# Mixture-of-experts stage: second blocks in four short branches, overflow in one branch at the end, a named ring of weights

## The chip, the core and the metric

The kernel runs on one core of a Trainium2 chip. The time is that of one execution on the device, in microseconds. Before the change it is 1266.83 us, the median of three runs (1257.88 to 1268.67).

## The reference

One layer of an encoder on 1024 tokens of width 1024, all in float32: differential attention, then a mixture of 16 experts, and a last RMSNorm. The change is in the experts:

```python
g_idx = jnp.argmax(g_logits, axis=-1)                       # one of 4 groups per token
top_v, top_i = lax.top_k(e_sel, EXPERT_TOP_K)               # 2 of its 4 experts
hid = jax.nn.silu(jnp.einsum('td,edf->tef', t, w_gate)) * jnp.einsum('td,edf->tef', t, w_up)
hid = hid * gates.astype(hid.dtype)[:, :, None]             # gate is 0 for experts not chosen
y = jnp.einsum('tef,efd->td', hid, w_down)
```

Each expert has three weights of 1024 x 512. A token's two experts add to one output row. Which tokens go to which expert is known only at run time; in all there are 2048 pairs of token and expert, and the routing of these inputs gives the experts 0 to 15: 102, 114, 97, 119, 153, 119, 191, 127, 98, 114, 103, 149, 153, 151, 133 and 125 tokens.

## The kernel before

**Stages.** Attention and routing fill the time up to about 763 us. The experts' stage follows, expert by expert, and at its end the last RMSNorm of all rows.

**Rows of tokens.** The normed tokens lie in DRAM as `h2d`, the residual sums as `accd`, each with 128 spare rows behind the 1024. `slots` and `slots_mm` make, two experts ahead, the list of row numbers of an expert (`idx`) and its gate weights (`tt`); a slot without a token gets a spare row's number. `gather` (an indirect DMA issued by POOL) fetches the rows of the first block (128 slots) and of the second (`M2` = 64 slots), `xpose` turns the first block into `XT`, and `scatter_add` adds the result to `accd`.

**Weights.** An expert's weights come in `NP` = 12 pieces of 128 x 1024 float32: 0 to 3 are the gate and up halves of the first 256 hidden columns, 4 to 7 of the other 256, 8 to 11 the down rows. `load_raw` has SP issue the load into one of `NRAW` raw tiles `wraw`. To multiply with nearly full precision, each piece is split: `split_hi` (ACT) casts it to `whi`, `split_lo` (DVE; pieces 8 and 11, the tuple `PLO`, on POOL) subtracts to give `wlo`. These lie in `NSLOT` = 14 pairs of tiles that the pool hands out in turn. Each split lets SP load the piece that is `NRAW` later.

**One expert.** `block` runs 48 matmuls of gate and up (`gu`) for the first 256 hidden columns, then 48 for the others; `gate` (ACT's SiLU, DVE's product) makes `sl`, `hid` transposes it on PE and splits it, `down` runs 12 matmuls per half into `py0` and `py1`. Work for other experts is put in by hooks, pairs of a count and a call: when the matmuls of `gu` reach that count, the call is written. `SPL` holds the counts of the splits, `EVAC` that of the previous expert's evacuation, `XPH`, `OH` and `SMM` those of the next experts' transposes and lists. ACT, DVE and POOL keep the order in which the calls are written, and PE too (`manual_schedule`); each engine works its own instructions in order and waits on semaphores for the others.

**The second block.** Where an expert has more than 128 tokens, its further ones (up to 64) run through the same weights with two terms instead of three, with hi and lo side by side in one 128-wide operand. This is one branch, `tc.If(n > P, label="small%d")`, taken by each engine for itself on the expert's count, and it is long: it holds the second block and the first block's down matmuls between its parts, and behind them `over_loop`, a loop over tokens past 192 in a branch of its own. The other side, `arm.Else()`, holds the first block's down matmuls alone. Two splits (`NARM`) stand in both sides, two more behind the branch. `mark_branch_hint_location` has PE told ahead where the branch is.

Of the kernel before, what the change touches and what calls it, by code (L numbers as in the profile page):

```python
# [35 lines left out]
def build(tc, x, c, ada_w, ada_b, norm_mix, norm_ffn, w_in, lq1, lk1, lq2, lk2, subln, w_out,  # L36
# [1027 lines left out]
    NRAW = 12  # L1064
# [34 lines left out]
    nslot = [0]  # L1099
# [39 lines left out]
    def split_done(n):  # L1139
# [43 lines left out]
    pos1, io1, pj, njn, mhalf, cnt, gates, oh = (RT0[n] for n in ("pos1", "io1", "pj", "njn", "mhalf", "cnt", "gates", "oh"))  # L1183
# [96 lines left out]
    def small_pe(xg):  # L1280
        pt = mps.tile([P, KT, M2], F32, name="xt", bufs=2)
# [95 lines left out]
    def gate(pg, g, R, lo=None):  # L1377
# [338 lines left out]
```

## Time and profile before

| | |
|---|---|
| Median of three runs | 1266.83 us |
| The profiled execution | 1261.08 us, span 1259.3 us, mean granted clock 0.955 |
| PE busy | 1115.3 us (89%) |
| DVE busy | 946.1 us (75%) |
| ACT, POOL busy | 733.6 us (58%), 383.5 us (30%) |
| Moved by DMA | 205.25 MB, mean 163 GB/s |

The profile has busy times of each engine, the waits with what ended them, and the instructions in order of time. PE is TensorE's matmuls and PEld its loads of weights, which overlap; PEldq, DVEq and so on are the sequencers, which branch, wait and issue. [...] Experts are counted from 0.

### The profile page before, as it was taken

What the parts mean: (1) busy time and instruction counts of PE and PEld (TensorE: products, weight loads), DVE (VectorE), ACT (ScalarE), POOL (GpSimd) and SP (SyncE); (2) the same over time, 40 slices, a digit from 0 to 9 for tenths busy, and PEclk for the clock granted to TensorE, in tenths of its full rate; (3) what the DMA queues carried; (4) which work ended last, traced back from release to release, by engine and by line L of the source; (5) the groups of instructions that cost most, each with busy time, mean ns of one, the idle gap of its engine ahead of it and who ended that gap; (6) DMA issues with size and microseconds to landing.
All of it is one profiled execution on the core that took longest, in us unless ns stands there. A gap on an engine that the chain in (4) does not pass through costs nothing. (4 is left out here: it accounts for less than half of the span.)

```text
span 1259.3 us, 18790 instructions
## 1 busy us (share of the span) xinstructions
PE 1115.3 (89%) x6760; PEld 926.5 (74%) x6760; DVE 946.1 (75%) x1500; ACT 733.6 (58%) x1220; POOL 383.5 (30%) x335
## 2 busy tenths in 40 slices
PE   4989999999999999998989967988898788898883
PEld 3657777777777777776778866877797677787772
DVE  5869788887889686789765477798777677677754
ACT  5566766666676667677554233666464555545544
POOL 3011110111111020115014125456364554545532
PEclk9899999999999999998999987999999998999996
DMA  9622033332223010124148536899797899679737
GB/s 329 196 67 64 26 91 91 92 93 80 88 89 93 30 37 15 42 66 129 69 125 284 172 130 215 276 317 344 200 314 225 271 292 321 185 218 267 199 101 273
DMA packets 153280, 205.25 MB, mean 163 GB/s; under 512 B 11652, under 2 KB 122917, under 8 KB 153138
## 3 DMA queue, kind: packets, MB, share of 16 engines
q1 hardware_dynamic: 146432, 179.86, 44.6%
q0 software_dynamic: 6512, 23.06, 7.7%
q8 instruction: 77, 1.26, 0.4%
q10 hardware_dynamic: 194, 0.54, 0.1%
q14 instruction: 65, 0.53, 0.1%
HBM read 175.77 MB, written 27.67 MB: 162 GB/s over the span
## 5 line engine op out<-in xcount | busy, mean ns | idle before, releaser
L1119 DVE TENSOR_TENSOR wlo<-wraw,whi 128x1024 fp32r<-128x1024 f32 x155 | 221.6, 1479 | 25.9 <-ACT whi L1114 15.4
L1373 PE MATMUL gu<-whi,XT 128*128 128x256 f32 x1216 | 211.1, 286 | 4.3 <-DVEq L1462 3.3
L1114 ACT CAST whi<-wraw 128x1024 fp32r<-128x1024 f32 x192 | 188.4, 1049 | 23.4 <-PE py L1405 17.8
L486 ACT ACTIVATE E<-E,mn 128x1024 f32<-128x1024 f32 x128 | 147.1, 1151 | 84.0 <-DVE mn L483 83.7
L1373 PEld LDWEIGHTS gu<-whi,XT 128*128 128x128 f32 x1216 | 175.6, 194 | 8.1 <-ACTq L1462 5.3
L483 DVE CUSTOM_DVE_ANT_0 E<-S,negd 128x1024 f32<-128x1024 f32 x128 | 152.8, 1220 | 19.3 <-PE S L478 18.6
L1373 PE MATMUL gu<-wlo,XT 128*128 128x256 f32 x704 | 152.0, 294 | 15.9 <-DVE wlo L1119 14.2
L143 POOL TENSOR_TENSOR wl<-wraw,wh 128x1024 fp32r<-128x1024 f32 x21 | 50.6, 2409 | 326.0 <-ACT wh L142 285.6
L285 PE MATMUL mm<-hH,wh 128*128 128x512 f32 x336 | 139.3, 415 | 2.1 <-DVE V L384 2.1
L285 PE MATMUL mm<-hL,wh 128*128 128x512 f32 x336 | 140.2, 417 | 0.0
L285 PE MATMUL mm<-hH,wl 128*128 128x512 f32 x336 | 138.7, 413 | 0.0
L1373 PEld LDWEIGHTS gu<-wlo,XT 128*128 128x128 f32 x704 | 111.6, 194 | 20.3 <-DVE wlo L1119 17.8
L1119 POOL TENSOR_TENSOR wlo<-wraw,whi 128x1024 fp32r<-128x1024 f32 x37 | 97.2, 2631 | 94.4 <-ACT whi L1114 94.4
L513 ACT CAST aH<-tp 128x512 fp32r<-128x512 f32 x128 | 74.0, 578 | 74.7 <-PE tp L511 74.4
L1405 PE MATMUL py<-whi,hid 128*128 128x512 f32 x256 | 96.2, 434 | 12.8 <-issue 10.2
L497 DVE SCALAR_TENSOR_TENSOR E<-E,r 128x1024 f32<-128x1024 f32 x64 | 85.8, 1341 | 27.8 <-ACT E L495 26.3
L514 DVE TENSOR_TENSOR aL<-tp,aH 128x512 fp32r<-128x512 f32 x128 | 88.0, 687 | 16.0 <-ACT aH L513 14.8
L511 PE MATMUL tp<-ident,E 128*128 128x128 f32 x512 | 78.6, 276 | 11.5 <-DVE aL L514 8.3
L511 PEld LDWEIGHTS tp<-ident,E 128*128 128x128 f32 x512 | 62.4, 142 | 35.0 <-DVE aL L514 15.4
L693 PE MATMUL mm<-wo,wh 128*128 128x512 f32 x240 | 80.1, 408 | 1.3 <-ACT mm L705 1.3
L285 PEld LDWEIGHTS mm<-hH,wh 128*128 128x128 f32 x336 | 63.4, 189 | 18.3 <-issue 5.1
L285 PEld LDWEIGHTS mm<-hL,wh 128*128 128x128 f32 x336 | 63.4, 189 | 17.1 <-issue 8.2
(346 smaller groups left out, 2337.8 us busy)
## 6 DMA issues: line engine op xcount, KB each, us to landing
wraw<-in_expert_w_gate SPq DMA_DIRECT2D x64, 512.0 KB
wraw<-in_expert_w_up SPq DMA_DIRECT2D x64, 512.0 KB
wraw<-in_expert_w_down SPq DMA_DIRECT2D x64, 512.0 KB
aw<-in_ada_w SPq DMA_DIRECT2D x64, 256.0 KB
wraw<-in_attn_w_in SPq DMA_DIRECT2D x23, 512.0 KB
ld<-in_ada_w SPq DMA_DIRECT2D x32, 256.0 KB
ld<-in_x SPq DMA_DIRECT2D x8, 512.0 KB
xt<-in_x SPq DMA_DIRECT2D x8, 512.0 KB
```

The costliest lines, as they stand in the source:

```text
L285: nc.tensor.matmul(pq, w[:, k], t[k][:, n], start=(k == 0 and i == 0), stop=(k == KT - 1 and i == 2))
L483: nc.vector.tensor_tensor_reduce(out=e, in0=sps[m], in1=negd[:, w0:w0 + S], op0=OP.add, op1=OP.min, scale=-slope, scalar=3.0e38, accum_out=mn)
L486: nc.scalar.activation(e, e, AF.Exp, bias=mn, scale=-1.0, accum_out=sm)
L497: nc.vector.scalar_tensor_tensor(es[0], es[1], r2, es[0], op0=OP.mult, op1=OP.add)
L511: nc.tensor.transpose(pt[:, i], a[:, k * P:(k + 1) * P], ident)
L513: nc.scalar.copy(th[:, kk * 4:kk * 4 + 4, q], pt)
L514: nc.vector.tensor_tensor(tl[:, kk * 4:kk * 4 + 4, q], pt, f(th[:, kk * 4:kk * 4 + 4, q]), op=OP.subtract)
L693: nc.tensor.matmul(py, w[:, h], wt[h][:, ns], start=(h == 0 and s == 0), stop=(h == H - 1 and s == 2))
L1114: nc.scalar.copy(WP[e, i][0], RAW[e, i])
L1119: eng.tensor_tensor(low, RAW[e, i], f(high), op=OP.subtract)
L1373: nc.tensor.matmul(pg[:, i], XT[:, xi, k], w[:, k % 4], start=(k == 0 and xi == 0 and wi == 0 and i == 0), stop=(k == KT - 1 and (xi, wi) ...
L1405: nc.tensor.matmul(py[n], hT[:, xi, i], WP[e, 8 + hf * 2 + i][wi][:, n * 512:(n + 1) * 512], start=(hf == 0 and j == 0), stop=(hf == 1 and ...
```

## The change

- The long branch goes. The first block's down matmuls, the splits and the evacuation stand outside any branch. The second block is cut into four short branches: its transposes (behind the gate/up matmuls), its first gate/up half (behind the first down half), its second gate/up half with the first down half (behind the second), and its second down half with the addition to `accd`, at the count `DSM` = 12 of the next expert. There is no other side and no hint.
- Six splits of the next expert stand between these branches, six at the counts of `SPL`; all low halves but two at the start of the stage are on DVE. The evacuation's second half moves from ACT and POOL to DVE.
- Tokens past 192 of all experts are one branch behind everything (`rest`), on the largest count `cmax`; it loads weights again and norms all rows again. The last expert's second block is `small15`.
- The slots are 14 named pairs in a list `RING`. Raw tiles are 11 instead of 12.
- Gathers and additions leave out slots whose row number is past 1023 (`bounds_check`). Counts in `OH`, `SMM`, `EVAC` and `N0` change.

```diff
-    NRAW = 12
+    NRAW = 11
     NRAW1 = 8
     NEARLY = 3
     CNT = 62
     XPH = (74, 86)
-    SMM = 80
-    OH = 40
-    NARM = 2
+    SMM = 92
+    OH = 66
...
+    RING = []
     def slot_tiles():
-        pool, nb = (mwr, NEARLY) if nslot[0] % NSLOT < NEARLY else (mw, NSLOT - NEARLY)
-        nslot[0] += 1
-        return [pool.tile([P, 1024], F32R, name=n, bufs=nb) for n in ("whi", "wlo")]
+        j = nheld[0] % NSLOT
+        if j == len(RING):
+            pool = mwr if j < NEARLY else mw
+            RING.append([pool.tile([P, 1024], F32R, name="%s%d" % (n, j)) for n in ("whi", "wlo")])
+        return RING[j]
...
-        eng = eng or (nc.gpsimd if i in PLO else nc.vector)
+        eng = eng or nc.vector
...
-    PLO = (8, 11)
-    EVAC = 52
-    N0 = 20
-    SPL = [(0, split_hi, 4), (0, split_lo, 4), (0, split_hi, 5), (0, split_lo, 5), (2, split_hi, 6), (3, split_hi, 7),
-           (30, split_lo, 6), (48, split_hi, 8), (48, split_lo, 8), (50, split_lo, 7), (50, split_hi, 10), (50, split_lo, 10),
-           (69, split_hi, 9), (70, split_lo, 9), (72, split_hi, 11), (80, split_lo, 11)]
+    EVAC = 60
+    DSM = 12
+    N0 = 28
+    SPL = [(0, 6), (24, 7), (56, 8), (64, 9), (80, 10), (90, 11)]
...
-    def gather(idx, b, tag, xg=None):
+    def gather(idx, b, xg=None):
         if xg is None:
-            xg = mg.tile([P, D], F32, name="xg" + tag, tag=tag)
-        m = M2 if b else P
-        nc.gpsimd.indirect_dma_start(out=xg[:m], out_offset=None, in_=h2d,
-                                     in_offset=bass.IndirectOffsetOnAxis(ap=idx[:m, b:b + 1], axis=0))
+            m, xg = (M2 if b else P), xg0[b]
+            nc.gpsimd.indirect_dma_start(out=xg[:m], out_offset=None, in_=h2d,
+                                         in_offset=bass.IndirectOffsetOnAxis(ap=idx[:m, b:b + 1], axis=0),
+                                         bounds_check=S - 1, oob_is_err=False)
+            return xg
...
-                                     in_=yo, in_offset=None, compute_op=OP.add)
-    def over_tiles(e):
-        if e < NE - 2:
-            return None, mp.tile([P, D], F32, name="yo")
-        return (mp.tile([P, D], F32, name="xc", tag="yo") if e == NE - 2 else raw_tile()), XG[e, 1]
-    def over_finish(e, ix, R, xc, yo):
-        if e < NE - 1:
-            scatter_add(ix[:R], yo[:R])
-        if e >= NE - 2:
-            xc, yo = xc[:R], yo[:R]
-            v.tensor_tensor(xc, xc, yo, op=OP.add)
-            sq = ss_tile()[:R]
-            nc.scalar.activation(yo, xc, AF.Square, accum_out=sq[:, 0:1])
-            r = rstd_of(sq, R)
-            v.scalar_tensor_tensor(xc, xc, r, nfin[0][:R], op0=OP.mult, op1=OP.mult)
-            out_rows(ix[:R], xc)
-    def over_block(e, XT, ix, g, R, lo=None):
-        xc, yo = over_tiles(e)
-        if xc is not None:
-            acc_rows(ix[:R], xc[:R])
+                                     in_=yo, in_offset=None, bounds_check=S - 1, oob_is_err=False,
+                                     compute_op=OP.add)
...
+    def small15(XT, ix, g):
+        e, R, xs = NE - 1, M2, XG[NE - 1, 1]
+        small_evac(small_pe(xs), XT)
+        xc = raw_tile()
+        acc_rows(ix, xc[:R])
+        block_steps(e, XT, g, R, xs, xs)
+        xc, yo = xc[:R], xs[:R]
+        v.tensor_tensor(xc, xc, yo, op=OP.add)
+        sq = ss_tile()[:R]
+        nc.scalar.activation(yo, xc, AF.Square, accum_out=sq[:, 0:1])
+        r = rstd_of(sq, R)
+        v.scalar_tensor_tensor(xc, xc, r, nfin[0][:R], op0=OP.mult, op1=OP.mult)
+        out_rows(ix, xc)
+    def rest(XT):
+        xl, yo = XG[NE - 1, 1], mp.tile([P, D], F32, name="yo")
+        for e in range(NE):
+            base = P + M2 if e < NE - 1 else 0
+            tc.no_sync_barrier()
+            with tc.If(cnts[e] > base):
+                for i in range(NP):
+                    load_raw(e, i)
+                    WP[e, i] = RING[i]
+                    nc.scalar.copy(RING[i][0], RAW[e, i])
+                    v.tensor_tensor(RING[i][1], RAW[e, i], f(RING[i][0]), op=OP.subtract)
+                v.memset(bs, float(base))
+                with tc.For_i(base, cnts[e], P):
+                    ix, tx = slots_mm(e, 1, slots(e, 1, base=bs))
+                    gather(ix, 0, xl)
+                    block_steps(e, run(xpose(xl, XT)), tx[:, 0, 3:4], P, yo)
+                    scatter_add(ix[:, 0:1], yo)
+                    v.tensor_scalar(bs, bs, float(P), None, op0=OP.add)
+        jk[0] = mp.tile([P, D], BF, name="jk", tag="hs")
+        for t in range(TB):
+            norm_load(t)
+            norm_sum(t)
+            rstds(t, t + 1)
+            norm_store(t)
...
+            tc.no_sync_barrier()
+            with tc.If(cnts[e] > P, label="small"):
+                small15(XT, idx[:M2, 1:2], tt[:, 1, 3:4])
+            tc.no_sync_barrier()
+            with tc.If(cnts[NE] > P + M2):
+                rest(XT)
+            return
+        upto(199)
-        tc.no_sync_barrier()
-        with tc.If(n > P, label="small%d" % e) as arm:
-            pt = small_pe(XG[e, 1])
-            g = tt[:, 1, 3:4]
-            xs = XG[e, 1]
-            if last:
...
-                s1 = gate(pg1, tt[:, 0, 3:4], P)
-                small_evac(pt, XT)
-                d = down(e, py, 0, h0, P)
-                take(d, 7)
-                h1 = hid(s1, P)
-                run(d)
-                spy = [mps.tile([P, 512], F32, name="spy%d" % n, tag="xt", bufs=2) for n in range(2)]
-                splits()
...
-                scatter_add(idx[:M2, 1:2], oyo[:M2])
-            over_loop(e, XT, n)
-        if last:
-            return
-        with arm.Else():
-            s1 = gate(pg1, tt[:, 0, 3:4], P)
-            d = down(e, py, 0, h0, P)
-            take(d, 7)
-            h1 = hid(s1, P)
-            splits()
...
+        g = tt[:, 1, 3:4]
+        xs = XG[e, 1]
+        def small(what):
+            tc.no_sync_barrier()
+            with tc.If(n > P):
+                what()
+        def splits(k):
+            split_to(nsplit[0] + k)
+        s1 = gate(pg1, tt[:, 0, 3:4], P)
+        pt = small_pt()
+        small(lambda: small_evac(small_pe(xs, pt), XT))
+        d = down(e, py, 0, h0, P)
+        take(d, 9)
+        h1 = hid(s1, P)
+        run(d)
+        splits(2)
+        sl, hs = mp.tile([P, 256], F32, name="sl"), mp.tile([P, 2, 2, P], F32R, name="hs")
+        pg = gu_tile()
+        small(lambda: gate(run(gu(e, XT, 0, M2, pg=pg)), g, M2, xs[:, 0:512], sl))
+        splits(2)
+        run(down(e, py, 1, h1, P))
+        pg2 = gu_tile("idx")
+        spy = [mps.tile([P, 512], F32, name="spy%d" % n, tag="xt", bufs=2) for n in range(2)]
+        def small_c():
+            hid(sl, M2, hT=hs)
+            gate(run(gu(e, XT, 1, M2, pg=pg2)), g, M2, xs[:, 512:1024], sl)
+            run(down(e, spy, 0, hs, M2))
+            hid(sl, M2, hT=hs)
+        def small_d():
+            for n in range(2):
+                run(down(e, spy, 1, hs, M2, (n,)))
+                fold(spy, oyo, n)
+                r = slice(n * 512, (n + 1) * 512)
+                v.tensor_tensor(oyo[:M2, r], oyo[:M2, r], g2b[:M2, r], op=OP.mult)
+            scatter_add(idx[:M2, 1:2], oyo[:M2])
+        small(small_c)
+        splits(2)
+        later.append((DSM, lambda: small(small_d)))
...
-            v.tensor_tensor(yo[:, 0:512], py[0], g2b[:, 0:512], op=OP.mult)
-            if e == NE - 2:
-                v.tensor_tensor(yo[:, 512:1024], py[1], g2b[:, 512:1024], op=OP.mult)
-            else:
-                nc.scalar.copy(yo[:, 512:1024], py[1])
-                nc.gpsimd.tensor_tensor(yo[:, 512:1024], yo[:, 512:1024], g2b[:, 512:1024], op=OP.mult)
+            for n in range(2):
+                v.tensor_tensor(yo[:, n * 512:(n + 1) * 512], py[n], g2b[:, n * 512:(n + 1) * 512], op=OP.mult)
...
-            tc.mark_branch_hint_location("small%d" % e, cnts[e] > P, engines=[mybir.EngineType.PE])
+            if e == NE - 1:
+                cnts[NE] = nc.values_load(cmax[0:1], min_val=0, max_val=S)
+                tc.mark_branch_hint_location("small", cnts[e] > P, engines=[mybir.EngineType.PE])
...
-            for c, what, i in SPL:
-                hooks.append((c, lambda e=e, i=i, what=what: what(e, i)))
-            hooks.append((SPL[-1][0], lambda: split_done(8)))
+            hooks += [(c, lambda: split_to(nsplit[0] + 1)) for c, i in SPL]
```

What moves, at three places. POOL, from the second gather of expert 1 to its next load of a count, first before (`wlo` is a weight's low half, `yo` the evacuated first block, `oyo` the second block's result):

```order
L1261 DMA xgxb<-h2d,ix 64x1024
L1119 TENSOR_TENSOR wlo<-wraw,whi 128x1024
L1577 TENSOR_TENSOR yo<-yo,g2b 128x512
L1419 DMA accd<-yo,ix 1152x1024
L1628 TENSOR_LOAD rk
```

and of the change:

```order
L1263 DMA xgxb<-h2d,ix 64x1024
L1540 COMPARE_AND_BRANCH
L1431 DMA accd<-oyo,ix 1152x1024
L1540 UNCONDITIONAL_BRANCH
L1540 ISA
L1540 UNCONDITIONAL_BRANCH
L1431 DMA accd<-yo,ix 1152x1024
L1631 TENSOR_LOAD rk
```

The split and the product are gone, and POOL passes a branch instead.

DVE, from the first block's second gate product of expert 0 (`sl`) into expert 1, before (the other side of the long branch):

```order
L1386 SCALAR_TENSOR_TENSOR sl<-sl,tt,gu 128x256
L1396 TENSOR_TENSOR hid<-tp,hid 128x256
L1119 TENSOR_TENSOR wlo<-wraw,whi 128x1024 x2
L1518 UNCONDITIONAL_BRANCH
L1119 TENSOR_TENSOR wlo<-wraw,whi 128x1024 x5
L1229 TENSOR_SCALAR rk<-rk 128x192 x8
L1386 SCALAR_TENSOR_TENSOR sl<-sl,tt,gu 128x256
L1119 TENSOR_TENSOR wlo<-wraw,whi 128x1024 x2
L1572 TENSOR_TENSOR yo<-py_7408,g2b 128x512
L1628 TENSOR_LOAD rk
L1396 TENSOR_TENSOR hid<-tp,hid 128x256
```

and of the change, from the same product:

```order
L1398 SCALAR_TENSOR_TENSOR sl<-sl,tt,gu 128x256
L1540 COMPARE_AND_BRANCH
L1299 TENSOR_TENSOR XT<-xt,XT 128x4x64 x2
L1540 UNCONDITIONAL_BRANCH x2
L1408 TENSOR_TENSOR hid<-tp,hid 128x256
L1122 TENSOR_TENSOR wlo_7650<-wraw,whi_7649 128x1024
L1122 TENSOR_TENSOR wlo_7656<-wraw,whi_7655 128x1024
L1540 COMPARE_AND_BRANCH
L1395 TENSOR_TENSOR xgxb<-xgxb,gu 64x512
L1398 SCALAR_TENSOR_TENSOR sl<-sl,tt,xgxb 64x256
L1540 UNCONDITIONAL_BRANCH x2
L1122 TENSOR_TENSOR wlo_6492<-wraw,whi_6491 128x1024
```

```order
L1122 TENSOR_TENSOR wlo_6500<-wraw,whi_6499 128x1024
L1122 TENSOR_TENSOR wlo_7291<-wraw,whi_7290 128x1024
L1122 TENSOR_TENSOR wlo_7294<-wraw,whi_7293 128x1024
L1540 COMPARE_AND_BRANCH
L1428 TENSOR_TENSOR oyo<-oyo,spy_7723 64x512
L1573 TENSOR_TENSOR oyo<-oyo,g2b 64x512
L1428 TENSOR_TENSOR oyo<-oyo,spy_7724 64x512
L1573 TENSOR_TENSOR oyo<-oyo,g2b 64x512
L1540 UNCONDITIONAL_BRANCH x2
L1122 TENSOR_TENSOR wlo_7297<-wraw,whi_7296 128x1024
L1398 SCALAR_TENSOR_TENSOR sl<-sl,tt,gu 128x256
L1122 TENSOR_TENSOR wlo_7389<-wraw,whi_7388 128x1024
```

Splits that stood behind one another now stand in pairs between the branches, and of the evacuation both halves are on DVE.

PE, from the last gate/up matmuls of expert 0 to the down matmuls, before and of the change (`xt` are the second block's transposes, `py` the down products):

```order
L1373 MATMUL gu<-wlo,XT 128x256 x2
L1373 MATMUL gu<-whi,XT 128x256 x2
L1518 COMPARE_AND_BRANCH
L1283 MATMUL xt<-ident,xgxb 128x64 x8
L1405 MATMUL py_7408<-whi,hid 128x512
```

```order
L1385 MATMUL gu<-whi_7388,XT 128x256
L1385 MATMUL gu<-whi_7392,XT 128x256
L1540 COMPARE_AND_BRANCH
L1292 MATMUL xt<-ident,xgxb 128x64 x8
L1540 UNCONDITIONAL_BRANCH x2
L1417 MATMUL py_7408<-whi_7434,hid 128x512
```

The first branch now ends behind the eight transposes; before, the down matmuls lay inside.

## Rows read from the trace of the kernel before

**Rows 1.** The page, busy us of each engine (share of the span)

```profile
PE 1115.3 (89%) x6760; PEld 926.5 (74%) x6760; DVE 946.1 (75%) x1500; ACT 733.6 (58%) x1220; POOL 383.5 (30%) x335
```

**Rows 2.** Nine stretches of the experts' stage: length, then busy us by engine

```profile
core 0: us, PE busy (x) PEld busy (x) DVE busy (x) ACT busy (x) POOL busy (x), PEclk, DMA share, GB/s
763.00:791.40 28.40, 23.08 (x151) 21.43 (x150) 18.83 (x23) 13.66 (x21) 15.92 (x23) 0.82 0.64 216
791.40:860.50 69.10, 59.94 (x445) 53.78 (x445) 59.57 (x76) 43.17 (x64) 41.04 (x39) 0.98 1.02 310
814.80:837.50 22.70, 19.53 (x149) 17.49 (x148) 20.99 (x26) 14.64 (x22) 12.30 (x12) 1.00 1.05 312
860.50:895.20 34.70, 31.97 (x241) 28.67 (x239) 24.95 (x35) 18.41 (x31) 14.10 (x14) 1.00 0.79 259
895.20:922.30 27.10, 22.68 (x148) 20.88 (x149) 21.41 (x26) 16.16 (x23) 18.30 (x16) 0.87 0.99 286
922.30:955.40 33.10, 31.92 (x241) 28.82 (x241) 22.42 (x35) 17.92 (x31) 15.50 (x13) 1.00 0.76 238
955.40:1062.60 107.20, 85.33 (x593) 76.50 (x593) 79.71 (x101) 59.03 (x86) 60.37 (x55) 0.90 0.97 293
1062.60:1208.80 146.20, 130.45 (x946) 116.68 (x944) 100.63 (x131) 76.03 (x122) 62.29 (x50) 0.99 0.74 213
763.00:1241.20 478.20, 408.77 (x2883) 366.41 (x2881) 346.13 (x442) 264.07 (x399) 244.09 (x219) 0.94 0.84 254
```

**Rows 3.** Waits of PE from 762 us: us in total, times, longest

```profile
PE tp L1392 <- DVE sl L1386: 18.8, 7, 3.8
PE gu L1373 <- DVE wlo L1119: 14.2, 14, 3.0
PE py L1405 <- issue: 10.2, 3, 4.5
PE py L1405 <- POOLq L1518: 9.3, 4, 5.8
PE py L1405 <- POOL wlo L1119: 4.1, 2, 2.5
PE gu L1373 <- DVEq L1462: 3.3, 5, 0.8
```

**Rows 4.** Branches of PE's sequencer, two lines: ns min/median/max

```profile
L1518 PEldq COMPARE_BRANCH  x16: 84/384/6532, 783.6 to 1237.1; - x16
L1462 PEldq COMPARE_BRANCH  x12: 187/354/3772, 891.3 to 1208.4; - x12
```

**Rows 5.** PE in order of time, expert 10: start, us, idle before

```profile
1054.13 0.77 PE L1405 MATMUL py<-whi,hid 128*128 128x512 f32 x1 [4.46 <-issue]
```

**Rows 6.** Waits of SP's queue, 762 to 1242 us

```profile
SPq L1093 <- DVEq L1462: 60.8, 5, 14.2
```

**Rows 7.** DVE in order of time, expert 3

```profile
836.26 6.99 DVE L1119 TENSOR_TENSOR wlo<-wraw,whi 128x1024 fp32r<-128x1024 f32 x6
...
844.99 5.30 DVE L1119 TENSOR_TENSOR wlo<-wraw,whi 128x1024 fp32r<-128x1024 f32 x2
```

**Rows 8.** POOL in order of time, expert 3

```profile
844.57 2.42 POOL L1119 TENSOR_TENSOR wlo<-wraw,whi 128x1024 fp32r<-128x1024 f32 x1 [5.20 <-ACT whi L1114]
846.94 2.27 POOL L1577 TENSOR_TENSOR yo<-yo,g2b 128x512 f32<-128x512 f32 x1
```

**Rows 9.** Groups by line: us, mean ns of one

```profile
L1572 DVE TENSOR_TENSOR yo<-py,g2b 128x512 f32<-128x512 f32 x15 | 10.2, 681 | 1.0 <-DMA xgxa<-h2d,ix 1.0
```

**Rows 10.** PE in order of time, end of expert 4's branch

```profile
894.01 0.63 PE L1405 MATMUL py<-whi,hid 128*128 128x512 f32 x2
895.24 0.47 PE L1373 MATMUL gu<-whi,XT 128*128 128x256 f32 x2 [0.60 <-DVEq L1462]
```

**Rows 11.** DMA queues, 814.8 to 860.5 us: packets, MB, share of 16 engines

```profile
q0 software_dynamic: 679, 2.45, 20.7%
```

**Rows 12.** POOL in order of time, the end

```profile
1252.37 1.06 POOL L1311 DMA_INDIRECT out<-yo,ix  x1 [7.87 <-POOLq L1518]
```

More of the change, by code (lines that the diff above doesn't have):

```diff
@@ L1182, in build @@
     v = nc.vector
-    pos1, io1, pj, njn, mhalf, cnt, gates, oh = (RT0[n] for n in ("pos1", "io1", "pj", "njn", "mhalf", "cnt", "gates", "oh"))
+    pos1, io1, pj, njn, mhalf, cnt, gates, oh, cmax = (RT0[n] for n in ("pos1", "io1", "pj", "njn", "mhalf", "cnt", "gates",
+                                                                        "oh", "cmax"))
     xg0 = [mg.tile([P, D], F32, name="xg" + n, tag=n) for n in ("xa", "xb")]
@@ L1278, in xpose, with small_pt, small_pe @@
         return XT
-    def small_pe(xg):
-        pt = mps.tile([P, KT, M2], F32, name="xt", bufs=2)
+    def small_pt():
+        return mps.tile([P, KT, M2], F32, name="xt", bufs=2)
+    def small_pe(xg, pt=None):
+        pt = small_pt() if pt is None else pt
         for k in range(KT):
@@ L1375, in gu, with gate @@
         return pg
-    def gate(pg, g, R, lo=None):
-        sl = mp.tile([P, 256], F32, name="sl")
+    def gate(pg, g, R, lo=None, sl=None):
+        sl = mp.tile([P, 256], F32, name="sl") if sl is None else sl
         if R == M2:
@@ L1456, in over_block @@
                 v.tensor_tensor(yo[:, r], py[n], g2b[:, r], op=OP.mult)
-        over_finish(e, ix, R, xc, yo)
-    def over_loop(e, XT, n):
-        tc.no_sync_barrier()
-        with tc.If(n > P + M2):
-            v.memset(bs, float(P + M2))
-            with tc.For_i(P + M2, n, P):
-                ix, tx = slots_mm(e, 1, slots(e, 1, base=bs))
-                xl = XG[e, 1]
-                gather(ix, 0, None, xl)
-                over_block(e, run(xpose(xl, XT)), ix[:, 0:1], tx[:, 0, 3:4], P)
-                v.tensor_scalar(bs, bs, float(P), None, op0=OP.add)
+    def small15(XT, ix, g):
[35 more added lines that the diff above has]
+            norm_store(t)
     def block(e, XT, idx, tt, hooks):
@@ L1505, in block @@
             finish15(ix, py, mp.tile([P, D], F32, name="yo"), XC[0])
-        else:
-            upto(199)
-        n = cnts[e]
-        nx = [divmod(j, NP) for j in range(nsplit[0], nsplit[0] + (0 if last else NARM))]
-        slots_to(nsplit[0] + len(nx))
-        def splits():
-            for j in nx:
-                split_hi(*j)
-                split_lo(*j)
-        tc.no_sync_barrier()
-        with tc.If(n > P, label="small%d" % e) as arm:
-            pt = small_pe(XG[e, 1])
-            g = tt[:, 1, 3:4]
-            xs = XG[e, 1]
-            if last:
-                small_evac(pt, XT)
-                over_block(e, XT, idx[:, 1:2], g, M2, xs)
-            else:
-                oyo = mp.tile([P, D], F32, name="yo") if e < NE - 2 else xs
-                s1 = gate(pg1, tt[:, 0, 3:4], P)
-                small_evac(pt, XT)
-                d = down(e, py, 0, h0, P)
-                take(d, 7)
-                h1 = hid(s1, P)
-                run(d)
-                spy = [mps.tile([P, 512], F32, name="spy%d" % n, tag="xt", bufs=2) for n in range(2)]
-                splits()
-                t0 = gate(run(gu(e, XT, 0, M2)), g, M2, xs[:, 0:512])
-                g1 = gu(e, XT, 1, M2, "idx")
-                take(g1, 24)
-                u0 = hid(t0, M2, "hs", 1)
-                t1 = gate(run(g1), g, M2, xs[:, 512:1024])
-                d = down(e, py, 1, h1, P)
-                run(down(e, spy, 0, u0, M2))
-                take(d, 4)
-                u1 = hid(t1, M2, "hs", 1)
-                take(d, 5)
-                run(down(e, spy, 1, u1, M2, (0,)))
-                fold(spy, oyo, 0)
-                run(down(e, spy, 1, u1, M2, (1,)))
-                fold(spy, oyo, 1)
-                run(d)
-                nc.gpsimd.tensor_tensor(oyo[:M2], oyo[:M2], g2b[:M2], op=OP.mult)
-                scatter_add(idx[:M2, 1:2], oyo[:M2])
-            over_loop(e, XT, n)
@@ L1553, in block @@
-        if last:
-            return
-        with arm.Else():
-            s1 = gate(pg1, tt[:, 0, 3:4], P)
-            d = down(e, py, 0, h0, P)
-            take(d, 7)
-            h1 = hid(s1, P)
-            splits()
-            run(d)
-            run(down(e, py, 1, h1, P))
-        split_done(NARM)
-        nx = [divmod(j, NP) for j in range(nsplit[0], nsplit[0] + (2 if e < NE - 2 else 0))]
-        for j in nx:
-            split_hi(*j)
-            split_lo(*j)
-        split_done(len(nx))
+            tc.no_sync_barrier()
```

35 lines of the change are left out of this document (19 added, 16 removed).

## Prediction

> **What bounds the kernel now.** I read the page first: PE is busy for 89% of the span [rows 1], and the chain of waits on it names only the last scatter, so it says nothing of the middle. Then I cut the experts' stage (763.0 to 1241.2 us) into one stretch per expert, by where a new expert's first gate/up matmul starts, and asked for busy times [rows 2]. The reader is to see three things. The stage takes 478.2 us, of which PE is busy 408.8: 69.4 us are idle. [...] The six with a second block last 34.7 + 33.1 + 146.2 = 214.0 us, of which expert 6 has 31.92 of PE work, 12.4 over an ordinary one. DVE and DMA stand close behind PE: in the third row DVE is busy 20.99 of 22.70 us and the DMA share is 1.05.
>
> So what can be won is PE's idle time and the clock. The waits of PE [rows 3] say who ends them: 18.8 us a transpose that waits for DVE's gate product, 14.2 a gate/up matmul that waits for DVE's low half of a weight, 9.3 + 4.1 a down matmul that waits for POOL (its skipped branch, and its two low halves per expert), 10.2 "issue", 3.3 the end of a small block's branch. "Issue" is the far jump over the small block: PE's sequencer needs 84 ns for the branch when it falls through and up to 6532 ns when it jumps [rows 4], and 4.46 us of one such jump stay visible [rows 5]. [...] And the loads of weights were held up by the long branch: SP's queue waited 60.8 us in five places for its end on DVE [rows 6].
>
> **The change, part by part.** *Far jump.* It is gone, with the Else side: -10.
>
> *POOL.* It splits no weights and multiplies no evacuation any more, so nobody waits there for it: -13. That work goes to DVE: two splits and a 512-wide product per expert. DVE's split takes 6.99/6 = 1.17 us by itself, but two of them took 5.30 us beside POOL's split and product, and POOL's run at the same time [rows 7, 8]. So DVE gets 2 x 1.17 + 0.68 [rows 9] = 3.0 us more and at least 5.30 - 2.33 = 3.0 us less: 21 us per ordinary expert, as now. ACT loses a copy and is not near the bound (14.64 us of 22.70).
>
> *Splits outside the branches.* Six of an expert's twelve splits now stand between the branches in the expert before, where loads follow each of them. What hangs on late DVE work is 18.8 + 14.2 = 33.0 us. I keep 8 of it: DVE at 21 us stays as full as PE, I count 0.4 us for each ordinary expert where PE reaches the second gate product before DVE does (an estimate from the order of the instructions), and 5 at both ends of the stage. That is -25; the bounds are 0 and -33.
>
> *Clock.* With no gap over 2.5 us left, the 11.7 us come back: -11.7. The first expert's clock is 0.82, but it starts out of idle time; nothing is counted.
>
> *End of the long branch.* -3.
>
> *Four skips.* Nine of experts 0 to 14 have no second block (those without a second-block matmul in the trace), so 36 branches are jumped. Each skipped body is replaced on PE, ACT and DVE by one instruction that waits for the engine's own last result. The nearest row is the skip of the old overflow loop at the end of a small block: the last down matmul pair runs from 894.01 to 894.64, the next matmul starts 0.60 us later [rows 10]; with the 0.16 us by which matmuls otherwise overlap, a skip costs PE 0.76 us. 36 x 0.76 = +27. The bounds: 0.25 (PE waits there anyhow for DVE) and 1.1 (as much again for the branch, median 0.354 us [rows 4]), so +9 to +40. [...]
>
> *Small block.* The same matmuls in the same number, 12.4 us on PE; the second half's transposes now come right after their gate product and stand uncovered: an estimate of 0.7 x 6 = +4 (0 to +8).
>
> *Fewer rows.* An ordinary expert moves 128 + 64 gathered and 128 added rows now. The reference's routing gives these experts 97 to 127 tokens, so about 218 rows stay. The software queue takes 20.7% of 16 engines' time over experts 2 and 3 (45.7 us), 4.7 us per expert [rows 11]; a third of it, 1.5 us, goes. I cost it at nothing: it brings the DMA from a share of 1.05 in 22.7 us to what fits in 22.4, which is what PE and DVE will need; without it DMA would be the bound at 23.8/1.05.
>
> *Ring, raw tiles.* The slots rotate as before; eleven raw tiles instead of twelve hold eleven twelfths of an expert, about 21 of 23 us, ahead. Nothing, as long as the DMA share stays under 1.05.
>
> *End.* The overflow of all experts is one branch behind everything, which is jumped on every engine; POOL's lies ahead of the last scatter's completion at 1252.37 [rows 12]. +3 (0 to +6.5, the longest jump).
>
> Sum: -10 -13 -25 -11.7 -3 +27 +4 +3 = -29. Counted by experts: ordinary ones 19.53 + 4 x 0.76 + 0.4 = 23.0, 8 of them 184 (-19); small ones 19.53 + 12.4 + 1.5 = 33.4, six of them 200 (-14); first and last +1: -32. I take -30. The profiled execution took 1261.1 us (span 1259.3), so 1231 for it; it lies 5.7 us under the median of the runs, 1266.8, which would give 1237. **I say 1234.**
>
> **Rivals.** *Slower: the short jumps fetch code.* If a jump on PE has to fetch its target, the sequencer needs 3.4 us and more (3772 and 6532 ns at most, medians 0.354 and 0.384, [rows 4]). Between two of the four branches stand only 12 down matmuls, some 2.8 us (two take 0.63 with 0.16 of overlap, so 0.235 each, [rows 10]), and the drain has emptied PE's queue: about 2.2 us of each fetch would show, and 2 us of clock behind it (11.7 us lost over some six gaps). If every third of the 36 jumps fetches (an assumption: the rows give medians and the longest alone), that is 12 x 4.2 = +50: 1234 + 50 = 1284. It decides from 10 jumps on. For it: four times as many branches. Against it: the bodies are short (8, 32, 44 and 8 matmuls, where the far jump passed over some 260). [...]
>
> *DVE stays late.* DVE too drains at four skips per ordinary expert, and it now has all splits; if the skips lengthen its cycle as they do PE's, the 33.0 us of waits stay: 1234 + 25 = 1259, no change that can be told. For it: DVE at 20.99 of 22.70 us. Against: its order puts a split of the next expert wherever it would idle.
>
> *The skips hide.* Where PE is jumped it may be about to wait for DVE anyway; at 0.25 us each the sum is 18 us less: 1216. [...] For it: the skip behind the gate/up matmuls stands where the gate product is due. Against: the row shows the gap with its matmul ready to go.
>
> *The change does not do what it says*, the overflow's branch being entered, is excluded: in expert 6, the fullest, PE ran no third block [rows 2].
>
> **How the numbers follow.** Forecast (1222 to 1250) 0.60; short jumps fetch 0.09; DVE stays late 0.17; skips hide 0.14. The range leaves out the first rival and half of the ends: 1206 to 1264. About 1% (12.7 us) is what can be told from no change; faster by more needs less than 1254. Faster: 0.60 + 0.14 + a quarter of 0.17 = 0.78; within 1%: the rest of it, 0.13; slower 0.09.
>
> **What would show it.** Ordinary experts of 22 to 24 us with a granted clock of 1.00 throughout, none of 27 or more; small ones of 33 to 34; on PE four gaps of some 0.6 us in each ordinary expert, ended by the skip; DVE's splits all near 1.2 us and POOL under 8 us per expert; no wait of SP for a branch's end. Wrong would be: gaps of PE over 2 us with "issue" behind the short branches, the transposes still waiting some 19 us for DVE's gate product, or ordinary experts at 25 us with the DMA share at 1.05.

## The result, and the profile after

The changed kernel takes 1223.10 us (median of four, 1222.29 to 1223.61) against 1263.05 for the kernel before (median of four, 1257.88 to 1268.67): a ratio of 0.968, 95% interval 0.963 to 0.973. I had said 1234. The two profiled executions differ by 38.5 us of span.

The page and stretches of the changed kernel, in the columns of [rows 1, 2]: experts 0; 1 to 3; 9; 4 to 7; 8 to 10; 11 to 14; 15 to its last matmul; and all.

```profile
PE 1108.1 (91%) x6760; PEld 916.9 (75%) x6760; DVE 939.6 (77%) x1560; ACT 727.8 (60%) x1206; POOL 265.2 (22%) x283
...
759.70:785.50 25.80, 23.40 (x150) 21.17 (x149) 17.02 (x27) 13.76 (x21) 11.69 (x20) 0.85 0.67 221
785.50:850.50 65.00, 60.80 (x444) 53.03 (x444) 58.27 (x85) 42.91 (x61) 22.28 (x30) 1.00 1.02 333
984.75:1006.50 21.75, 20.31 (x148) 17.74 (x149) 19.51 (x29) 14.39 (x21) 7.41 (x10) 1.00 1.06 347
850.50:962.70 112.20, 106.39 (x776) 94.75 (x776) 89.78 (x136) 65.47 (x101) 30.61 (x42) 0.98 0.85 261
962.70:1028.20 65.50, 61.20 (x444) 53.34 (x444) 58.66 (x85) 43.45 (x61) 21.86 (x30) 1.00 1.05 344
1028.20:1164.90 136.70, 130.85 (x952) 117.96 (x953) 100.95 (x151) 74.85 (x119) 29.27 (x35) 0.98 0.73 224
1164.90:1198.10 33.20, 20.05 (x118) 17.12 (x116) 19.00 (x23) 18.10 (x29) 9.59 (x10) 0.79 0.62 206
759.70:1198.10 438.40, 402.69 (x2882) 357.37 (x2880) 343.68 (x503) 258.53 (x387) 125.31 (x167) 0.96 0.84 266
```

The reader is to see the length of an ordinary expert (one without a second block: 1 to 3, 5 and 7 to 10): (65.00 + 65.50)/6 = 21.75 us. Eight of them make 174; before, they took 69.10 + 27.10 + 107.20 = 203.4 [rows 2], 25.4 each: -29.4. What is left of experts 4 to 7 and 11 to 14 is 112.2 + 136.7 - 2 x 21.75 = 205.4 for six with a second block, 34.2 each, before 214.0: -8.6. The first expert gives -2.6, the start of the stage -3.3 (`norms_behind` below, with the same work ahead of the stage, starts it at 762.6, so this is no effect of the change). Expert 15 to the end of the span takes 55.9 us, before 50.5: +5.4. The sum is -38.5.

Waits of PE and SP from 759 us, and the branches on PE (columns of [rows 3, 4]):

```profile
PE tp L1404 <- DVE sl L1398: 16.1, 7, 12.7
PE tp L1404 <- DVEq L1540: 5.9, 8, 0.8
PE xt L1292 <- PE gu L1385: 5.1, 6, 0.9
...
SPq L1359 <- DMA accd<-oyo,ix: 26.7, 1, 26.7
SPq L1093 <- DVEq L1540: 20.0, 27, 0.8
...
L1540 PEldq COMPARE_BRANCH  x84: 70/179/434, 777.5 to 1163.6; - x84
L1530 PEldq COMPARE_BRANCH  x1: 3862/3862/3862, 1198.3 to 1198.3; - x1
```

None of the 84 branch instructions of the short branches (60 branches, of which the 24 that are entered have two each) took PE longer than 0.43 us; the one far jump left on PE, over the overflow's branch, took 3.9 us behind PE's last matmul. SP's loads wait for no branch longer than 0.8 us (60.8 us in five waits before [rows 6]). Then expert 9 on PE and on DVE, in order of time:

```profile
998.42 0.40 PE L1385 MATMUL gu<-whi,XT 128*128 128x256 f32 x2
998.97 0.47 PE L1417 MATMUL py<-whi,hid 128*128 128x512 f32 x1
999.27 0.39 PE L1417 MATMUL py<-wlo,hid 128*128 128x512 f32 x1
...
1000.67 0.39 PE L1417 MATMUL py<-wlo,hid 128*128 128x512 f32 x1
1001.81 0.44 PE L1404 MATMUL tp<-ident,sl 128*128 128x128 f32 x2 [0.75 <-DVEq L1540]
...
1002.55 0.62 PE L1417 MATMUL py<-whi,hid 128*128 128x512 f32 x2
1003.32 0.47 PE L1417 MATMUL py<-whi,hid 128*128 128x512 f32 x1
1003.62 0.40 PE L1417 MATMUL py<-wlo,hid 128*128 128x512 f32 x1
```

```profile
1000.15 1.21 DVE L1122 TENSOR_TENSOR wlo<-wraw,whi 128x1024 fp32r<-128x1024 f32 x1
1001.29 0.47 DVE L1398 SCALAR_TENSOR_TENSOR sl<-sl,tt,gu 128x256 f32<-128x256 f32 x1
```

A skip stands at 1003.32: 1002.55 + 0.62 = 1003.17, so 0.15 us of idle. The matmul behind it starts 0.54 us after the one before, 0.30 more than the 0.235 of its neighbours, and the next one 0.07 late: **0.38 us a skip**. The one wait of the expert is at 1001.81, for a gate product that stands behind a split on DVE.

### The profile page after: what moved, and what is told of

Its sections match the earlier page's. It is cut to its first block, busy times and chain, and to the rows that moved or that the text cites. A ratio compares the mean times of both kernels' runs of the same rounds, so it can differ in the third digit from the quotient of the medians.

```text
span 1220.8 us, 19162 instructions
## 1 busy us (share of the span) xinstructions
PE 1108.1 (91%) x6760; PEld 916.9 (75%) x6760; DVE 939.6 (77%) x1560; ACT 727.8 (60%) x1206; POOL 265.2 (22%) x283
## 5 line engine op out<-in xcount | busy, mean ns | idle before, releaser
L1122 DVE TENSOR_TENSOR wlo<-wraw,whi 128x1024 fp32r<-128x1024 f32 x187 | 224.9, 1231 | 33.2 <-ACT whi L1117 22.9
L1117 ACT CAST whi<-wraw 128x1024 fp32r<-128x1024 f32 x192 | 193.4, 1049 | 6.4 <-ACTq L1540 4.7
L1385 PEld LDWEIGHTS gu<-whi,XT 128*128 128x128 f32 x1216 | 172.3, 191 | 10.0 <-issue 5.8
L1385 PE MATMUL gu<-wlo,XT 128*128 128x256 f32 x704 | 148.1, 289 | 2.0 <-POOL wlo L1122 2.0
L1417 PE MATMUL py<-whi,hid 128*128 128x512 f32 x256 | 93.3, 426 | 3.2 <-ACT hid L1407 0.5
L511 PE MATMUL tp<-ident,E 128*128 128x128 f32 x512 | 79.2, 278 | 10.2 <-DVE aL L514 7.2
L285 PEld LDWEIGHTS mm<-hH,wl 128*128 128x128 f32 x336 | 63.4, 189 | 17.1 <-issue 7.9
```

What stands on the lines that cost most here:

```text
L285: nc.tensor.matmul(pq, w[:, k], t[k][:, n], start=(k == 0 and i == 0), stop=(k == KT - 1 and i == 2))
L511: nc.tensor.transpose(pt[:, i], a[:, k * P:(k + 1) * P], ident)
L1117: nc.scalar.copy(WP[e, i][0], RAW[e, i])
L1385: nc.tensor.matmul(pg[:, i], XT[:, xi, k], w[:, k % 4], start=(k == 0 and xi == 0 and wi == 0 and i == 0), stop=(k == KT - 1 and (xi, wi) ...
L1417: nc.tensor.matmul(py[n], hT[:, xi, i], WP[e, 8 + hf * 2 + i][wi][:, n * 512:(n + 1) * 512], start=(hf == 0 and j == 0), stop=(hf == 1 and ...
```

## The experiments

Each is the changed kernel with one edit, unless it says otherwise; times are compared with its 1223.1 us, which was run on another occasion, so 2 to 3 us between them say nothing. Ratios are against the kernel before, run beside them; its median was 1254.5 to 1263.1 us on these occasions, which alone moves a ratio by up to 0.007.

**What a skip costs.** The fourth branch in eight:

```diff
+            take(gens[0], 1)
...
+        later.append((1, lambda: small(one)))
+        for j in range(6):
+            later.append((2 + j, lambda: small(lambda: take(gens[0], 1))))
...
         later.append((DSM, lambda: small(small_d)))
```

The first seven have one matmul each, `small_d` has the last one and the rest.

> The changed kernel, but its fourth short branch (second down half and addition) is eight branches: seven of one matmul each, one behind each of the first gate/up matmuls of the next expert, and one with the rest. Nine of the fifteen experts skip them all, so 63 more skips on PE. If a skip costs PE 0.76 us, as the prediction took it: 63 x 0.76 = +48, 1271 us. If it costs what the gaps of the changed kernel's trace show, 0.38 us from start to start: +24, 1247. [...] The 42 branches that are entered may add some us to each. I expect 1247 to 1255.

Measured: 1267.9 us, ratio 1.009 (1.004 to 1.013). Experts 2 and 9:

```profile
813.12:840.17 27.05, 24.79 (x148) 20.86 (x149) 19.67 (x29) 14.36 (x21) 7.42 (x10) 0.87 0.88 271
1015.28:1039.55 24.27, 22.03 (x148) 18.34 (x149) 19.68 (x29) 14.34 (x21) 7.41 (x10) 1.00 0.98 300
```

At a granted clock of 1.00 (a share of full speed, PEclk) seven more skips cost 24.27 - 21.75 = 2.5 us, 0.36 each, close to the 0.38 of the gaps. In expert 2, at 0.87, they cost 5.3 (experts 1 and 3 are within 0.3 us of it, at the same clock): the short gaps took the clock down too. So the +45 is neither price alone (63 x 0.36 = 23); why experts 9 and 10 kept the clock, and what the branches that are entered add, stays open.

**What a long jump costs.** A branch that is never entered behind the third one, with 240 matmuls (`far_skip`) and with 96 (`mid_skip`, `range(2)`):

```diff
         small(small_c)
+        tc.no_sync_barrier()
+        with tc.If(n > P + M2):
+            for _ in range(5):
+                run(gu(e, XT, 1, P, pg=pg2))
         splits(2)
```

> The changed kernel with a branch that is never entered in each of the experts 0 to 14, behind the third short branch; its body is 240 matmuls, about as long as the side that was jumped before. If the length of the jump is what costs (the prediction's far jump, 1.8 to 6.5 us of PE's sequencer of which up to 4.46 us showed, with clock behind it): 15 x 2 to 15 x 4.5 = +30 to +67, 1253 to 1290. If a jump costs the same 0.38 us whatever its length: 15 x 0.38 = +6, 1229. I expect 1255 or more, with branch times of PE above 1.5 us for these and not for the short ones.

> As the run with a branch of 240 matmuls that is never entered in each of the experts 0 to 14, but with a body of 96 matmuls (each with its load of weights). There each jump took PE's sequencer 5.1 to 6.6 us, where the four short ones take 0.07 to 0.43. If every longer jump fetches: 15 x 6.8 = +102, 1325. If it is the length that decides, and 192 instructions lie within reach: 15 x 0.38 = +6, 1229. I expect 1229 to 1232.

Measured: 1325.1 us (1.055, 1.049 to 1.060) and 1240.1 us (0.985, 0.982 to 0.989). The added branches on PE, first those of 240, then of 96:

```profile
L1578 PEldq COMPARE_BRANCH  x15: 1453/5117/6246, 786.6 to 1265.2; - x15
```

```profile
L1578 PEldq COMPARE_BRANCH  x15: 208/371/1520, 786.8 to 1177.8; - x15
```

PE's waits behind the jumps of 240, and an ordinary expert there:

```profile
PE gu L1385 <- PEq L1578: 69.2, 14, 6.6
...
1049.06:1079.22 30.16, 22.79 (x148) 20.14 (x149) 19.76 (x28) 14.42 (x20) 7.61 (x10) 0.84 0.79 238
```

Between these two, which differ in nothing else, the length decides. Over 240 matmuls no jump took less than 1.45 us (the longest 6.25, the median 5.1; the expectation for 96 puts each at 5.1 to 6.6), PE stood 69.2 us in 14 waits, and an expert behind one ran at 0.84 to 0.92: +102. Over 96, twelve of 15 stayed under 0.45 us and three took 1.5: +17. With a load of weights per matmul the two bodies are 480 and 192 instructions; at what length between them a jump becomes dear, and what in it takes the time, was not shown. The three slower jumps over 96 are not told by length alone.

What these two runs leave out is the hint. The kernel before had PE told ahead of its branch, and of its nine far jumps in experts 0 to 10 three took 0.37 to 0.44 us and six 1.8 to 6.5. So a hint may be worth something on PE; no run tried it on one of these jumps.

**POOL's share.** Given back to it in the changed kernel, and taken from it in the kernel before (there with `PLO = ()`, the product on DVE):

```diff
-        eng = eng or nc.vector
+        eng = eng or (nc.gpsimd if i in PLO else nc.vector)
...
+    PLO = (8, 11)
...
+            nc.scalar.copy(yo[:, 512:1024], py[1])
+            nc.gpsimd.tensor_tensor(yo[:, 512:1024], yo[:, 512:1024], g2b[:, 512:1024], op=OP.mult)
```

> The changed kernel with POOL's share given back: low halves of pieces 8 and 11 on POOL, the second half of the evacuation copied by ACT and multiplied by POOL. By the prediction's term (PE waited 13 us for POOL, and DVE's splits take 2.65 instead of 1.17 us beside it) it should be slower by about 13: 1236. Rival: DVE is relieved of 3 us per expert, and the wait of 0.75 us for the gate product in each expert goes: 1213. Second rival: both hidden, 1223. I expect 1230 to 1236, with DVE splits above 1.4 us in the mean and waits of PE for POOL again.

> The kernel before with one part of the change: POOL splits no weights and multiplies no evacuation but at the start and the end, DVE does it. By the prediction (PE's 13 us of waits on POOL go, DVE's 3 us more and 3 us less cancel) it should be faster by 13 or a little more. Rival: in the order of before DVE's two splits more stand behind the branch and PE waits for them instead: no change, within 1%. Second rival, from the run with POOL's share given back (67 us slower than the changed kernel): POOL's work is worth far more than 13, so -30 and more. I expect -5 to -20.

Measured: 1290.2 us (1.028, 1.022 to 1.033), and for the second 1244.4 us (0.990, 0.986 to 0.994), 13.5 under the kernel before (8 to 17 by the interval). So the size of 13 came out there, but not from the waits that I had named. PE's waits in that run, to be read against [rows 3]:

```profile
PE gu L1373 <- DVE wlo L1119: 11.3, 19, 3.0
PE xt L1283 <- issue: 10.9, 6, 2.5
PE tp L1392 <- DVE sl L1386: 6.3, 10, 1.2
PE py L1405 <- DVE sl L1386: 6.2, 2, 3.3
PE py L1405 <- issue: 5.9, 3, 4.1
...
PE py L1405 <- POOL wlo L1119: 4.1, 2, 2.5
```

The 9.3 us behind POOL's branch are gone. The 4.1 us for its low halves are still there: both waits lie in expert 15, where POOL splits in this run too. The waits for DVE's products and low halves fell from 33.0 to 23.8 us, and those called "issue" rose from 12.3 (the 10.2 of [rows 3] and 2.1 for `xt`) to 16.8.

In the new order POOL's share is 67 us, which I had not expected: DVE and the waits of PE with it given back,

```profile
844.97 5.62 DVE L1232 TENSOR_SCALAR rk<-rk 128x192 bf16<-128x192 bf16 x8
...
PE idx L1244 <- DVE rk L1232: 37.9, 14, 3.4
```

and DVE's same eight in a run with no split or product of POOL beside them (`product_first`, below):

```profile
991.02 1.66 DVE L1231 TENSOR_SCALAR rk<-rk 128x192 bf16<-128x192 bf16 x8
```

The lists' comparisons, now at count 66, fall beside POOL's product and split. They do not run slower one by one: the median of the eight stays at 0.26 us in every expert, but in 11 of 14 experts one of them takes 2.4 to 3.7 us. In the row above one of 1.3 us ends with POOL's product (846.2) and one of 3.5 with POOL's split (850.5). PE waits for them up to 3.4 us, and its clock falls (0.87 over expert 3, 0.90 over the stage, where the changed kernel has 0.96). The splits on DVE rose from 1.23 to 1.44 us in the mean, with the median at 1.22 in both: here too a few are held. What holds the single ones was not shown. How the 67 us divide between these waits, the clock and the rest was not measured.

**Rows moved.** Both `bounds_check` arguments taken out.

> The changed kernel with gathers and additions that move every slot's row again, spare rows too (no bound on row numbers). The prediction cost the fewer rows at nothing in themselves, but said that without them DMA, at a share of 1.05 in 22.7 us, would be the bound at 22.7 us per ordinary expert (now 21.7): +1 us in each of nine, +9, 1232. If the weights' loads still come in time with the raw tiles' lead: 1223. I expect 1223 to 1229.

Measured: 1226.0 us (0.976, 0.972 to 0.981). Experts 8 to 10 take 65.5 us as in the changed kernel:

```profile
965.53:1031.05 65.52, 61.25 (x444) 53.45 (x445) 58.71 (x85) 43.44 (x61) 21.90 (x30) 1.00 1.07 338
```

In this profile the experts' stage starts 2.7 us later (762.4 instead of 759.7), and from there to expert 14 it is 1 us shorter, so the 2.9 us between the medians are not the experts'. The fewer rows are worth nothing here, and at a DMA share of 1.07 the loads do not yet set the time.

**Where the splits stand.** The six between the branches all behind the third (`splits(2)` twice removed, `splits(6)` there).

> The changed kernel with the six splits that stand between the short branches (two behind the first, second and third one) all behind the third. It undoes the prediction's term of -25 for splits that stand where the loads and DVE can keep up. By that size: 1223 + 25 = 1248. By the order alone the next expert's first gate/up matmul then waits for a cast and two low halves, 1.05 + 2 x 1.2 less what lies beside, some 3 us in each of 15 experts, and a gap over 2.5 us costs clock too: +45 to +60, 1268 to 1283. Rival: DVE (19.5 busy of 21.7 us) makes it up: 1223. I expect 1265 to 1285, the wait on PE being for the low half of a weight at the start of an expert.

Measured: 1256.6 us (0.998, 0.996 to 1.000). Expert 5 with the third and fourth branch of expert 4, then experts 8 to 10, and below them the first of the two in the changed kernel:

```profile
878.65:914.47 35.82, 31.37 (x200) 26.85 (x199) 25.95 (x39) 20.20 (x30) 10.19 (x12) 0.90 0.68 200
976.08:1041.20 65.12, 60.98 (x444) 53.28 (x445) 58.40 (x86) 43.13 (x61) 23.23 (x31) 1.00 1.04 339
...
877.60:907.25 29.65, 27.89 (x200) 24.27 (x199) 23.56 (x37) 17.32 (x27) 8.37 (x11) 1.00 0.68 202
```

Ordinary experts lose nothing: with the branches skipped, "behind the third" is the same place. The stretch that holds expert 4's second half goes from 29.65 us to 35.82, those behind experts 6, 11, 12 and 13 likewise by 6 to 8, in short waits for casts and low halves (1.9 and 0.7 us here) and in clock (0.90 instead of 1.00). So to stand between the branches and not behind the third pays for the experts with a second block only; I had put the 25 us on all. What it is worth that the splits have left the long branch, this run does not tell: it does not bring that branch back.

**The gate product and the end.** The twelfth split behind the first branch (`product_first`), the first norm sums at count 200 (`norms_behind`), and no overflow branch (`no_rest`: `rest` and its `tc.If` taken out):

```diff
         small(lambda: small_evac(small_pe(xs, pt), XT))
+        if e:
+            splits(1)
...
+            hooks += [(c, lambda: split_to(nsplit[0] + 1)) for c, i in SPL[:-1]]
...
-           (80, norm_sum, 0), (80, norm_sum, 1), (80, rstds, 0, 2), (90, norm_store, 0),
-           (90, norm_sum, 2), (90, norm_sum, 3), (90, rstds, 2, 4), (200, norm_store, 1), ...
+           (200, norm_sum, 0), (200, norm_sum, 1), (200, rstds, 0, 2), (200, norm_store, 0),
+           (200, norm_sum, 2), (200, norm_sum, 3), (200, rstds, 2, 4), (200, norm_store, 1), ...
```

> The changed kernel; in experts 1 to 14 the twelfth split stands behind the first short branch instead of at count 90, so behind the second gate product on DVE and not ahead of it. In the trace of the changed kernel the SiLU is done at 998.99, DVE splits until 1001.12 and the product comes at 1001.04, PE waits 0.75 us for it in each expert (0.9 from start to start). If that split is what makes it late, -0.9 x 14 = -12, 1211. Rival: DVE (19.5 of 21.7 us) or the loads (DMA share 1.05) are the bound and the wait moves to another place: 1220 to 1223. I expect 1211 to 1216, with ordinary experts at 20.9 us.

> The changed kernel; at the last expert the sums of squares of rows 0 to 511 (counts 80 and 90) stand behind the gate/up matmuls (count 200) as all the others do. The wait of 12.7 us on PE for the second gate product came from ACT, which stood 8.3 us in such a sum, before the last split and the SiLU, until the rows had been read back behind the last addition. If so, the wait goes and PE ends some 10 to 12 us earlier; the end is then set by reading, summing and storing the rows, which begins at 1180 as before: the first expert rows' finish on DVE comes at 1195 instead of 1203, -8, 1215. Rival: the reading of the rows sets the end alone: 1223. I expect 1213 to 1219.

> The changed kernel without the branch for tokens past 192 at its end, which is never entered here (left out: tokens past 192 of an expert, of which these inputs have none). The prediction put that branch at +3 (0 to +6.5). In the trace of the changed kernel the last addition's issue on POOL is followed by 3.2 us in which POOL does nothing behind this branch and by one more count of its queue (1.27 us); the span ends 11.8 us behind the last issue, before it was 6.7. If the branch is the cause: -5, 1218, 6.7 us from the last issue to the end. Rival: the 11.8 us come from the landing of the last rows: 1223. I expect 1218.

Measured: 1213.0 us (0.964, 0.961 to 0.968); 1225.2 (0.974, 0.971 to 0.977); 1218.5 (0.969, 0.966 to 0.973). With the product first, experts 8 to 10 take 62.57 us, 20.9 each, and no wait of PE for DVE is left in them:

```profile
958.83:1021.40 62.57, 60.58 (x444) 53.69 (x445) 58.65 (x85) 43.73 (x61) 22.42 (x31) 1.00 1.07 349
```

DVE, busy for 58.65 of 62.57 us, was no bound. The norms' sums were the wrong suspect: with them moved PE ended 12 us earlier (1185.8 instead of 1198.1) and the span did not. What sets the end is the way of the last rows in the changed kernel,

```profile
1168.00 2.30 POOL L1431 DMA_INDIRECT accd<-yo,ix  x1 [21.47 <-DVE yo L1583]
1175.66 2.41 POOL L1431 DMA_INDIRECT accd<-oyo,ix  x1 [5.36 <-DVE hid L1408]
...
1179.98 4.42 SPq L1359 DMA_DIRECT2D wraw<-accd  x8
...
1208.68 1.07 POOL L1320 DMA_INDIRECT out<-yo,ix  x1 [7.87 <-SPq L1530]
```

two additions one behind the other (6.9 us from issue to landing of the first kind), the reading back behind both, and 12.1 us from the last scatter to the end of the span (1220.8). Without the overflow's branch these 12.1 are 7.1 (its last scatter, below, to 1216.9), before they were 6.9 [rows 12].

```profile
1209.84 1.07 POOL L1320 DMA_INDIRECT out<-yo,ix  x1 [7.87 <-ACTq L1527]
```

**All of it.** The first two edits together and, for expert 14, the evacuation right behind its down matmuls and the fourth branch right behind the third (`all_tail`); then, by the last line, POOL told ahead of the last branch (`all_tail_hint`):

```diff
         run(down(e, py, 1, h1, P))
+        if e == NE - 2:
+            evac()
...
         small(small_c)
+        if e == NE - 2:
+            small(small_d)
...
+                tc.mark_branch_hint_location("rest", cnts[NE] > P + M2, engines=[mybir.EngineType.Pool])
```

> The changed kernel with the gate product ahead of the twelfth split (alone 1213), the norms' first sums behind the gate/up matmuls (alone no gain, PE done 12 us earlier) and, for expert 14, the evacuation of its first block right behind its down matmuls and the fourth branch right behind the third. In the changed kernel the first block's addition is issued at 1168.0, the second block's waits for its landing and is issued at 1175.7, the rows are read back from 1180.0. With the first one issued some 10 us earlier, the second one waits for its own product alone (some 1169.5) and the reading starts at 1174, -6: 1213 - 6 = 1207. Rival: the last product on PE then sets the end, or the reading takes as long as it is shared with the weights' loads: 1211 to 1213. I expect 1205 to 1209.

> The run with the three changes of order (1207.4 us), and POOL told ahead, some 40 us before its end, whether the last branch will be entered. There POOL did nothing for 3.2 us behind that branch. If those are the fetch of the jump's target and the hint brings it ahead: -3, 1204. Rival: the hint does nothing on POOL, or its own instructions on POOL cost as much: 1207. I expect 1204 to 1207.

Measured: **1207.4 us** (0.961, 0.958 to 0.963), 15.7 under the changed kernel, and 1209.3 with the hint (0.960, 0.957 to 0.963). The end of the first:

```profile
1149.84 1.57 POOL L1431 DMA_INDIRECT accd<-yo,ix  x1 [12.98 <-DVE hs L1408]
1158.61 5.58 POOL L1431 DMA_INDIRECT accd<-oyo,ix  x1 [7.21 <-DVE oyo L1584]
...
1166.30 4.04 SPq L1359 DMA_DIRECT2D wraw<-accd  x8
...
1193.19 1.07 POOL L1320 DMA_INDIRECT out<-yo,ix  x1 [7.86 <-ACTq L1527]
```

The second addition now waits for its product, not for the first one's landing. From the first gate/up matmul of expert 14's third branch to the last scatter it is 47.0 us, in the changed kernel and in `product_first` 52.7; counted from there, the first addition goes out 8.4 us earlier than in the changed kernel. Of the 5.7 us, 3.9 lie before the rows are read back, which is the order of the two additions; 1.8 lie behind it, where the norms' sums were moved (in `norms_behind` that part is 1.4 us shorter too). Whether the hint helps stays open: behind the jump POOL's next instruction came 0.8 us later instead of 3.2, and from the last scatter to the end of the span it is 10.7 us instead of 12.1, but the time did not fall.

## Why the prediction was right, and where it was not

The time lies 1.1 us inside the range. With the skips at the price that they had, the sum would have given some 1220, below it: the direction and most of the terms were right, that the range held is in part luck.

- **Four skips, +27: the step that was mis-sized.** They cost 36 x 0.38 = +14. I took the price from a skip whose row names its releaser, "0.60 <-DVEq" [rows 10]: the profile has PE wait there for DVE's passage through the branch, and I read it as PE's own drain. The time came out between the forecast (1234) and the rival in which skips hide (1216).
- **The work of an ordinary expert, 19.53 us.** It was too much as a floor: the stretch it came from has 3.17 us idle in three waits (22.70 less 19.53 [rows 2]), and each leaves some 0.23 us of lost overlap in PE's busy time (0.16 of overlap and 0.07 at the restart, taken from the rows at 1003.32). The work alone is then, as an estimate, 18.8. With four skips of 0.38 and 0.9 for the gate product (0.4 forecast) that is 21.2 of the 21.75 measured; forecast 23.0. Most of the rest is in the 16 matmuls of the lists, which take 0.9 to 1.2 us and took 0.70.
- **Far jump, -10; clock, -11.7.** Right in kind: ordinary experts run at 1.00, and far jumps put in cost both things at once. Neither size was measured alone. The 11.7 are PE's work in the eight ordinary experts, 59.94 + 22.68 + 85.33 = 168.0 us [rows 2], over 8 x 19.53; no run shows them by themselves. What the trace of before shows is the granted clock behind the gaps: between 800 and 1208 us it fell to 0.50 at each of PE's seven gaps of 2.77 us and more (0.50 over 1054.1 to 1059.1, behind the 4.46 us of [rows 5]) and at none of those up to 2.51. In the changed kernel 2.5 us is no bound: in experts 4, 11 and 13 the clock is 0.60 to 0.68 over the 4 to 5 us from the first branch's transposes on, behind a wait of no more than 0.9 us.
- **POOL, -13.** The size came out in the order of before (13.5 measured), in part by luck: 9.3 of the waits went as forecast, the 4.1 stayed, and waits for DVE went in their place, where I had DVE's gain and loss cancel. That the same share costs 67 in the new order was not foreseen: the terms of a sum hold for one order only.
- **Late DVE work, 8 of 33.0 us left.** 5.9 us are left in the eight ordinary experts (3.4 more in the six others are counted with the small block), none for low halves; the 12.7 at the end were not on the path. The reason I gave was wrong: DVE is not too full, one split stood ahead of the product (-10 with it moved). The -25 as such was not measured alone.
- **Fewer rows, 0.** Right, but my condition was not: at a DMA share of 1.07 and 21.8 us PE waits for no load of weights.
- **Small block, +4.** 1.5 us of waits in each, 8.5: the transposes of the first branch (0.9) and of the second half (0.57). 34.2 us each, forecast 33.4.
- **End, +3.** 5.2 in the profile, 4.6 in the medians, on POOL, behind the last scatter, with nothing left to hide it.
- **Ring and eleven raw tiles, 0.** Not tried alone.
- **Short jumps fetch (1284).** Refuted: at most 434 ns. Over 96 matmuls three jumps of 15 took 1.5 us, over 240 all took that or more. The medians of 0.354 and 0.384 us that I worked with mix branches that fall through with branches that jump; the nine far jumps of experts 0 to 10 alone have a median of 3.0.
- **DVE stays late (1259).** Refuted by the ordinary experts' 21.75 us.

## What to carry to other kernels

A branch that is jumped was cheap here (0.4 us of PE) while its body was short (up to 44 matmuls) and it was not followed closely by others; over a body of 240 matmuls, without a hint, the jump itself took 1.45 to 6.25 us and the expert behind it ran at a clock of 0.84 to 0.92. Before a gap is used as a price, read its releaser: a wait for another engine is not the price of the instruction that stands there. At the end of a program look at who waits for whose landing, not at the longest idle time: 12.7 us of PE's waiting were worth nothing, an addition that went out 8 us earlier was worth 4.

## What the runs showed of the hardware

- The far jump of 240 matmuls took PE 1.5 to 6.2 us, ACT and DVE 45 to 63 ns where their own bodies were empty: in `far_skip` only the engine with the long body paid.
- Beside POOL's splits and products single instructions of DVE are held and the others are not slowed: of eight bfloat16 comparisons one takes up to 3.7 us and the median 0.26 (`pool_share`), so the eight take 5.62 us instead of 1.66; of DVE's float32 splits the mean goes from 1.23 to 1.44 us and the median stays at 1.22.
- Seven more gaps of 0.15 us, one between any two matmuls, left PE's granted clock at 1.00 in two experts, at 0.93 in one and took it to 0.87 over three others (`d_in_eight`); the four of the change left it at 1.00 in all ordinary experts.
